# One weight block for the input and forget gates, and modulation sums that leave TensorE as columns

## The chip, the cores and the metric

The kernel runs on one core of one Trainium2 chip. The metric is the device time in microseconds (us) of one execution; three runs of the kernel before give 1740.52 us in the median (1740.15 to 1742.07).

## The reference

One step of a diffusion backbone with one layer on T = 640 tokens (128 of context, 512 latent) of D = 1024 features. What matters here is the modulation and the mixer's first product:

```python
mod = jax.nn.silu(cond) @ w_mod + b_mod            # cond: c for the latent tokens, c_ctx for the context
sh1, sc1, g1, shm, scm, gm, sh2, sc2, g2 = jnp.split(mod, N_MOD, axis=-1)
h = modulate(rmsnorm(x, norm_g[0]), sh1, sc1)
x = x + 0.5 * g1[:, None, :] * swiglu(h, ffn1_w1, ffn1_w2)
h = modulate(rmsnorm(x, norm_g[1]), shm, scm)
y, C, n, m = mixer(h, ...)                         # z = h @ w_in + b_in, 9232 columns
x = x + gm[:, None, :] * y
h = modulate(rmsnorm(x, norm_g[2]), sh2, sc2)
x = x + 0.5 * g2[:, None, :] * swiglu(h, ffn2_w1, ffn2_w2)
```

In `z`, 8 columns are the input gates (2 directions x 4 heads) and the 8 after them the forget gates. They feed the scans of the mLSTM; the other columns are q, k, v and o per head, the short convolution's inputs and two output gates.

## The kernel before

Everything is feature-major: x is eight tiles of 128 features x 640 tokens, and the tokens are worked in two halves of 320. TensorE (PE) does nearly all of it in products of 128 x 128 weights and 128 x 320 activations. For precision each operand is split into a high and a low part, so one product is three matmuls (`three`, L235 to L240: high*high, high*low, low*high). A block of 128 weight columns over 1024 rows thus costs 8 x 2 x 3 = 48 matmuls. Weights come by DMA from SyncE's queue (SP) into a ring of five raw tiles `wr` (L544 for the modulation, L195 for the rest, L1052 for the gates); ScalarE (ACT) casts the high part `wh` (L73) and VectorE (DVE) subtracts to the low part `wl` (L74), some four half-blocks ahead of their use. Sums of blocks `ws` (L211) are for Strassen's form, in which a pair of blocks takes seven products in place of eight (`pair_el`).

The program is a list of elements run in order; each engine executes its own instructions in the order in which the elements emit them. The parts that the change touches:

**Head of the mixer** (`head_el`, L340). Behind the second norm come three pairs of column blocks without Strassen: the two gate blocks (8 real columns each, the other 120 zeroed by GpSimd and loaded as four small DMAs, `gate_load`), then q and k of head 0. The left halves of the first three blocks are interleaved; then come the modulation products that `mid` holds (L582); then the right halves of these three blocks, then both halves of the other three. While PE does these, DVE and ACT make the sums and splits for Strassen's form of the same activations (the list `work`, 28 calls, L842 to L851 and L74), spread evenly over the units behind the first. The gates leave PSUM by `gate_ev` (L1083), one bias per partition; `gate0` and what follows, woven into the next four pairs, turn them into decays on DVE and ACT.

**Modulation on VectorE** (`mod_dve`, L649). Ten half-channels (512 columns of `w_mod`, two condition vectors) are computed by DVE: `acc += w * cm` (L668) into two accumulators per half (128 partitions x 512, or two pieces of 256), spread over other elements by `with_units`. The sum over partitions is then made by PE in four steps, an element apart: `red` (L676) multiplies each accumulator, as the moving operand, by two columns of the constant `sel`, giving two rows of 512 in PSUM; `mod_cols` copies them to SBUF (`rows_`, L557, two DVE copies), turns them into columns by four transposes on PE (`turn`, L562), and adds the bias (`put_`, L568) into `modT`. Half-channels whose products PE does itself (L582, L604, L629) go through `mod_cols` too.

In row names `ax` and `ps` are PSUM banks, `ma`, `x` and `HT1h`/`HT2h` the accumulators, `H..h`/`H..l` and `U..` split activations, `t` temporaries.

Of the kernel before, what the change touches and what calls it, by code (L numbers as in the profile page):

```python
# [44 lines left out]
def mixer_step(ctx: ExitStack, tc: tile.TileContext, x_prompt, x_sample, state_C, state_n, state_m,  # L45
# [30 lines left out]
    # ------------------------------------------------------------ program: weights run ahead of their use  # L76
# [122 lines left out]
    # ------------------------------------------------------------ products  # L199
    # One pair of 128-column blocks of weights against both token halves: seven products (Winograd's form  # L200
    # of Strassen's algorithm over column blocks, halves of the contraction and halves of the tokens).
# [46 lines left out]
    def relax(left=1):  # L248
        """Emit what can wait no longer, with this many calls to come."""
        while lazy and len(lazy) >= left:  # L250
            lazy.pop(0)()
# [46 lines left out]
    def pair_el(load1, load2, ev, e1=None, units=(), spare_v=False):  # L298
        """units: elements with operands of their own, put between the products."""
        po = pair_ops(e1=e1)  # L300
        at_ = {1 + 2 * i: u for i, u in enumerate(units)}
        loads, ops_ = [load1, load2], []
        for i, name in enumerate(ORDER):
            ops_.append(po[name])
            if i in at_:
                ops_ += [dict(o, raws=[len(loads)], src=(lambda t, c: lambda o: rtile[o["base"] + t][:, c:c + 512])(
                    len(loads), c)) for c, o in zip((0, 512), at_[i]["ops"])]
                loads += at_[i]["raws"]

        def emit():  # L310
            nf = len(fill)
            for i, _ in enumerate(pair_steps(ORDER, ev, spare_v)):
                if i in at_:
                    at_[i]["emit"]()
                relax(7 - i)
                drain(nf - nf * (i + 1) // 7)
        return dict(element(loads, ops_, emit), pair=True)
# [22 lines left out]
    def head_el(p, chain, work, mid=()):  # L340
        """The three pairs behind a norm, without Strassen: three left halves first, row block by row block as the
        norm yields them, then what mid holds, while the right halves are made."""
        pre = len(mid) // 2
        order = [None] * pre + [0, 1, 2] + [None] * (len(mid) - pre) + [3, 4, 5]
        at_ = {t: i for i, t in enumerate(order) if t is not None}

        def emit():
            flush()
            n = {"i": 0}

            def take(u, i):
                u["emit"](raw(el["base"] + i))
                rdone.add(el["base"] + i)
                load_more()

            def some(*_):
                n["i"] += 1
                if n["i"] == 3 and soon:
                    soon.pop(0)()
                while len(work) > 0 and n["i"] * total >= 18 * (total - len(work) + 1):  # L360
                    work.pop(0)()

            total = len(work)
            ev = lambda t: lambda h_, ps: p[t // 2][2](t % 2, h_, ps)
            hold()
            for i in range(pre):
                take(mid[i], i)
            w = [[op()] for t in range(3)]
            ps = [big() for t in range(3)]
            for k in range(KT):  # L370
                if k == 4:
                    for t in range(3):
                        w[t].append(op())
                for t in range(3):
                    three(ps[t][:, :HT], *w[t][k // 4], k % 4, plain_acts(k, 0), k == 0, k == KT - 1)
                if k == 3:
                    chain[0]()
                if k == 4:
                    chain[1]()
            for t in range(3):  # L380
                ev(t)(0, ps[t][:, :HT])
            chain[2]()
            for i in range(pre, len(mid)):
                take(mid[i], 3 + i)
            chain[3]()
            for t in range(3):
                unit(w[t], KT, plain_acts, 1, ev(t), {3: some, 7: some})
                release(2)
            for t in range(3, 6):
                w = [op(), op()]  # L390
                unit(w, KT, plain_acts, 0, ev(t), {3: some, 7: some})
                unit(w, KT, plain_acts, 1, ev(t), {3: some, 7: some})
            while work:
                work.pop(0)()
            for f in chain[4:]:
                f()
        loads = [p[t // 2][t % 2] for t in range(6)]
        loads = [u["raws"][0] for u in mid[:pre]] + loads[:3] + [u["raws"][0] for u in mid[pre:]] + loads[3:]
        oa = [dict(tile_ops(KT, at_[t])[i], raws=[at_[t]]) for i in range(2) for t in range(3)]
        ob = [dict(o, raws=[at_[t]]) for t in range(3, 6) for o in tile_ops(KT, at_[t])]  # L400
        el = dict(element(loads, oa + ob, emit), calm=True)
        return el

    def halves_el(loads, nk, acts, ev, after):
        """Column blocks whose left halves all come first, then their right halves."""
# [54 lines left out]
    # ------------------------------------------------------------ constants  # L460
# [15 lines left out]
    sel = cst.tile([P, 4], F32, name="sel")  # L476
    G.memset(sel, 0.0)
    G.memset(sel[:, 0:1], 1.0)
    G.memset(sel[:, 3:4], 1.0)
# [17 lines left out]
    gb = cst.tile([36, 2], F32, name="gb")  # L497
# [3 lines left out]
    for d in range(2):  # L501
        for i, off in enumerate((IG_OFF, FG_OFF)):
            G.dma_start(gb[32 * d:32 * d + 4, i:i + 1], dap(b_in, off + 4 * d, [[1, 4], [1, 1]]))
        G.dma_start(m0[32 * d:32 * d + 4, :], dap(state_m, 4 * d, [[1, 4], [1, 1]]))

    # Sums seeded by a copy into PSUM go on accumulating: every bank they use has been written by the PE once.
# [32 lines left out]
    # ------------------------------------------------------------ modulation  # L539
# [9 lines left out]
    def mod_cols(ch, m0_, n, p, parts):  # L549
        """Rows of the modulation to columns, in three steps."""  # L550
# [64 lines left out]
    def mod_mix(ch, half):  # L615
        """Half of a channel: units with split operands and units in float32 by turns."""
# [33 lines left out]
    def mod_dve(ch, halves, wide):  # L650
        units = []
        for half in halves:
            hold_ = {}
            for kq in range(4):
# [16 lines left out]
                def red(hold_=hold_):  # L671
                    p = aux()
                    n = 512 // len(hold_[0])
                    for j in range(len(hold_[0])):
                        for i in range(2):
                            PE.matmul(p[:2, j * n:j * n + n], sel[:, 2 * i:2 * i + 2], hold_[i][j], start=(i == 0),  # L676
                                      stop=(i == 1))
                    hold_["p"] = p

                def fin(ch=ch, half=half, hold_=hold_):  # L680
                    hold_["f"] = mod_cols(ch, 4 * half, 4, hold_["p"][:2, :], 1)
                    hold_["f"].pop(0)()

                def more(hold_=hold_):
                    hold_["f"].pop(0)()
                units.append((mod_load(ch, half, kq), fns, [red, fin, more, more] if kq == 3 else []))
        return units

    def with_units(main, units, spare=0):
        """Spread modulation units over elements; what a unit leaves to be done follows an element later."""  # L690
# [37 lines left out]
    # ------------------------------------------------------------ norms  # L728
# [87 lines left out]
    def right_chain(n, sh, first=False):  # L816
        """Steps in the order of head_el, and the sums of Strassen's algorithm that it makes by the way."""
# [63 lines left out]
    # ------------------------------------------------------------ feed-forward  # L881
    GROUPS = (6, 6, 6, 4)

    def ffn(w1, w2, g, norm_, lists, units, e1=None, mid=()):
        """Elements: [head], then per group the other pairs and the column blocks of w2."""
        head, els, f0 = [], [], 0
        for size in GROUPS:
            U = {}
            grp = []
            for j in range(size):  # L890
# [15 lines left out]
                if f0 + j < 3:  # L906
                    head.append(p)
# [28 lines left out]
    # ------------------------------------------------------------ start: x, first norm  # L936
# [83 lines left out]
    # ------------------------------------------------------------ mixer  # L1020
# [26 lines left out]
    def gate_load(off):  # L1047
        def load(t):
            G.memset(t, 0.0)
            r3_ = t.rearrange("p (k n) -> p k n", k=KT)  # L1050
            for d in range(2):
                nc.sync.dma_start(r3_[:, :, 32 * d:32 * d + 4],  # L1052
                                  dap(w_in, off + 4 * d, [[IN_COLS, P], [P * IN_COLS, KT], [1, 4]]))
        return load
# [25 lines left out]
    def gate_ev(mi, h, src):  # L1080
        if (mi, h) == (0, 0):
            GT["t"] = tp.tile([P, T], F32, name="sqacc")
        V.tensor_scalar(GT["t"][64 * mi:64 * mi + 36, hsl(h)], src[0:36, :], gb[:, mi:mi + 1], None, op0=OP.add)  # L1083
# [154 lines left out]
    def head_steps(h):  # L1238
# [103 lines left out]
        def rs_begin():  # L1342
            """The mean squares to the power -0.5, by Newton's iteration from an estimate on the bits."""
# [118 lines left out]
    prog.append(head_el([(gate_load(IG_OFF), gate_load(FG_OFF), gate_ev), h0[0], h0[1]], chain, work,  # L1462
# [16 lines left out]
    # ------------------------------------------------------------ output side of the mixer  # L1479
# [138 lines left out]
    # ------------------------------------------------------------ second feed-forward, output  # L1618
# [92 lines left out]
```

## Time and profile before

| | |
|---|---|
| median of 3 runs | 1740.52 us |
| the profiled execution: span from its first to its last instruction (the profile shows no other time of it) | 1743.3 us |
| PE busy | 1706.1 us, 98% of the span |
| PE weight loads | 1625.3 us, 93% |
| DVE busy | 1299.9 us, 75% |
| ACT busy | 814.4 us, 47% |
| mean granted TensorE clock | 0.995 |

Matmuls are pipelined: the duration of one in the profile is longer than the distance from its start to the next one's start, so costs on PE are read from starts, not from durations. The records of one fp32 matmul with an unsplit operand are two (18 calls of L757 are 36 records), each with its own weight load.

### The profile page before, as it was taken

The page shows a single profiled execution, that of the slowest core. Times are in us where ns is not written, and L with a number is a line of the kernel's source. Part 1 is how long each engine was busy: PE and PEld are TensorE (multiplying, and loading weights), DVE is VectorE, ACT ScalarE, POOL GpSimd, SP SyncE. Part 2 cuts the span into 40 slices and gives each one's busy share as a digit, 9 for nine tenths or more (in the row PEclk, how much of TensorE's full clock was granted, in tenths as well). Part 3 has the DMA queues.
Part 4 walks back from the last instruction along what each step waited for, and adds up shares of the span by engine and source line. Part 5 has one row for each costly group of instructions (what it writes and reads, how often), then busy time and mean ns, then how long its engine had stood idle before and what let it go on. Part 6 is the DMA issues. An engine that isn't in the chain of part 4 may idle for free.

```text
span 1743.3 us, 29445 instructions
## 1 busy us (share of the span) xinstructions
PE 1706.1 (98%) x11169; PEld 1625.3 (93%) x11169; DVE 1299.9 (75%) x2742; ACT 814.4 (47%) x1749; POOL 169.5 (10%) x253
## 2 busy tenths in 40 slices
PE   8899999999999999999999999999999999999997
PEld 3889999999989899999999999999989999999997
DVE  5787787786868868787887788869767567467476
ACT  5553352452554675564653255542255435245253
POOL 1010000000030122111102222001100000000001
PEclk9899999999999999999999999999999999999999
DMA  8335334343343443333328433347432322322222
GB/s 290 100 116 150 86 112 119 97 116 115 95 111 112 99 115 82 88 101 78 105 87 270 145 85 86 99 142 217 136 94 62 101 73 68 103 73 85 82 77 61
DMA packets 273501, 193.13 MB, mean 111 GB/s; under 512 B 12179, under 2 KB 248346, under 8 KB 273360
## 3 DMA queue, kind: packets, MB, share of 16 engines
q1 hardware_dynamic: 264112, 161.96, 32.1%
q0 software_dynamic: 8480, 28.63, 5.9%
q8 instruction: 88, 1.44, 0.4%
q10 hardware_dynamic: 768, 0.66, 0.1%
q14 instruction: 53, 0.43, 0.1%
HBM read 175.92 MB, written 15.31 MB: 110 GB/s over the span
## 4 chain that ended last, share of the span: by engine, by line
PE 82%; DVE 8%; ACT 5%; issue 3%; DMA 2%; POOL 0%; ACTq 0%; DVEq 0%; POOLq 0%
PE ps L238 25%; PE ps L239 25%; PE ps L240 25%; DVE wl L74 2%; ACT wh L73 1%; PE ax L1292 1%; PE ax L1323 1%; PE ax L676 1%; DMA wr<-in_w_mod_dram 1%; PE ax L1295 1%; PE ax L582 1%; DVE ws L211 1%; DVE t L1436 1%; DVE x L1448 0%; PE ax L1269 0%
## 5 line engine op out<-in xcount | busy, mean ns | idle before, releaser
L74 DVE TENSOR_TENSOR wl<-wr,wh 128x512 fp32r<-128x512 f32 (+1 forms) x444 | 290.9, 671 | 96.2 <-ACT wh L73 94.3
L73 ACT CAST wh<-wr 128x512 fp32r<-128x512 f32 (+1 forms) x444 | 258.5, 595 | 195.8 <-PE ps L239 159.0
L74 DVE TENSOR_TENSOR wl<-ws,wh 128x512 fp32r<-128x512 f32 x288 | 202.8, 705 | 62.0 <-ACT wh L73 61.5
L73 ACT CAST wh<-ws 128x512 fp32r<-128x512 f32 x288 | 175.0, 618 | 105.7 <-DVE ws L211 63.9
L238 PE MATMUL ps<-Uh,wh 128*128 128x320 f32 x704 | 218.7, 311 | 0.0
L239 PE MATMUL ps<-Ul,wh 128*128 128x320 f32 x704 | 217.1, 308 | 0.0
L240 PE MATMUL ps<-Uh,wl 128*128 128x320 f32 x704 | 217.0, 308 | 0.0
L870 DVE SCALAR_TENSOR_TENSOR x<-ps,modT,x 128x128 f32<-128x128 f32 (+2 forms) x216 | 82.7, 433 | 121.8 <-PE ps L240 121.8
L238 PEld LDWEIGHTS ps<-Uh,wh 128*128 128x128 f32 x704 | 132.1, 188 | 2.6 <-issue 2.6
L238 PE MATMUL ps<-HT4h,wh 128*128 128x320 f32 x392 | 124.6, 318 | 8.2 <-ACT t L284 3.6
L239 PEld LDWEIGHTS ps<-Ul,wh 128*128 128x128 f32 x704 | 132.1, 188 | 0.2 <-DVE Ul L74 0.2
L240 PEld LDWEIGHTS ps<-Uh,wl 128*128 128x128 f32 x704 | 132.1, 188 | 0.0
L238 PE MATMUL ps<-H11h,wh 128*128 128x320 f32 x392 | 124.2, 317 | 1.7 <-ACT H11h L73 1.7
L239 PE MATMUL ps<-HT4l,wh 128*128 128x320 f32 x392 | 122.2, 312 | 0.7 <-DVE HT4l L74 0.7
L239 PE MATMUL ps<-H11l,wh 128*128 128x320 f32 x392 | 122.4, 312 | 0.1
L238 PE MATMUL ps<-H21h,wh 128*128 128x320 f32 x392 | 122.4, 312 | 0.0
L240 PE MATMUL ps<-H11h,wl 128*128 128x320 f32 x392 | 122.1, 311 | 0.0
L240 PE MATMUL ps<-HT4h,wl 128*128 128x320 f32 x392 | 122.1, 311 | 0.0
L240 PE MATMUL ps<-H21h,wl 128*128 128x320 f32 x392 | 121.3, 310 | 0.2 <-DVE wl L74 0.2
L239 PE MATMUL ps<-H21l,wh 128*128 128x320 f32 x392 | 121.1, 309 | 0.0
L238 PE MATMUL ps<-H22h,wh 128*128 128x320 f32 x360 | 113.0, 314 | 0.0
L240 PE MATMUL ps<-H22h,wl 128*128 128x320 f32 x360 | 111.7, 310 | 0.0
(380 smaller groups left out, 4560.0 us busy)
## 6 DMA issues: line engine op xcount, KB each, us to landing
wr<-in_ffn_w_dram SPq DMA_DIRECT2D x88, 512.0 KB, 3.9
wr<-in_w_mod_dram SPq DMA_DIRECT2D x72, 512.0 KB, 3.8
wr<-in_w_in_dram SPq DMA_DIRECT2D x72, 512.0 KB, 3.9
wr<-in_ffn_w_dram SPq DMA_DIRECT2D x48, 384.0 KB, 3.5
wr<-in_ffn_w_dram SPq DMA_DIRECT2D x16, 256.0 KB, 2.9
wr<-in_w_ml_out_dram SPq DMA_DIRECT2D x8, 512.0 KB, 5.0
wr<-in_w_sc_out_dram SPq DMA_DIRECT2D x8, 512.0 KB, 4.1
wr<-in_w_o_dram SPq DMA_DIRECT2D x8, 512.0 KB, 4.5
```

The costliest lines, as they stand in the source:

```text
L73: A.copy(hi, raw)
L74: V.tensor_sub(lo, raw, f32(hi))
L211: getattr(engine, fn)(t, part(o, a), part(o, b))
L238: PE.matmul(ps, hi[:, ws], ah, start=start, stop=False, skip_group_check=True)
L239: PE.matmul(ps, hi[:, ws], al, start=False, stop=False, skip_group_check=True)
L240: PE.matmul(ps, lo[:, ws], ah, start=False, stop=stop, skip_group_check=True)
L582: PE.matmul(hold["p"][:2, :], cm[:, 2 * kq + k, :], w[:, 512 * k:512 * k + 512], start=(kq == 0 and k == 0), stop=(kq == 3 and k == 1))
L676: PE.matmul(p[:2, j * n:j * n + n], sel[:, 2 * i:2 * i + 2], hold_[i][j], start=(i == 0), stop=(i == 1))
L870: V.scalar_tensor_tensor(X[m][:, o + a:o + b], ps[:, a:b], modT[:, g, m, cd:cd + 1], X[m][:, o + a:o + b], op0=OP.mult, op1=OP.add)
L1292: PE.matmul(p2[:, :DH + 1], S["q", dt][:, sl], S["C"][d][:, dt, :], start=(dt == 0), stop=(dt == 1))
L1295: PE.matmul(p1[:, :DH + 1], S["p", ch][:, d, :], PO["vt"][:, ch, :], start=True, stop=True)
L1323: PE.matmul(p[:, :DH + 1], kw[:, dt * P:(dt + 1) * P], PO["vt"][:, ch, :], start=True, stop=True)
```

## The change

Two edits.

*Gates.* One weight tile holds both gate blocks: the input gates of the two directions in columns 0 and 32, the forget gates in columns 64 and 96. `head_el` takes a list of single blocks, here the gate block and the four of q and k, and spreads `work` over the units that are left (`points = 4 * nb - 6`: 14 for five blocks, 18 for six). The gates leave PSUM in one instruction per half, 100 partitions tall, with `gb` a single column.

*Modulation.* In `mod_dve` each 128-column piece of an accumulator becomes the stationary operand, and one column of ones the moving one: eight matmuls give a [128, 8] result that is already in columns. `sel`, the copies and the transposes go, and `fin` adds the bias straight from PSUM.

```diff
-    def head_el(p, chain, work, mid=()):
-        pre = len(mid) // 2
-        order = [None] * pre + [0, 1, 2] + [None] * (len(mid) - pre) + [3, 4, 5]
+    def head_el(blocks, chain, work, mid=()):
+        pre, nb = len(mid) // 2, len(blocks)
+        order = [None] * pre + [0, 1, 2] + [None] * (len(mid) - pre) + list(range(3, nb))
+        points = 4 * nb - 6
...
-                while len(work) > 0 and n["i"] * total >= 18 * (total - len(work) + 1):
+                while len(work) > 0 and n["i"] * total >= points * (total - len(work) + 1):
                     work.pop(0)()
...
-            for t in range(3, 6):
+            for t in range(3, nb):
                 w = [op(), op()]
                 unit(w, KT, plain_acts, 0, ev(t), {3: some, 7: some})
                 unit(w, KT, plain_acts, 1, ev(t), {3: some, 7: some})
...
-    gb = cst.tile([36, 2], F32, name="gb")
+    gb = cst.tile([100, 1], F32, name="gb")
...
                 def red(hold_=hold_):
-                    p = aux()
+                    p = hold_["p"] = aux()
                     n = 512 // len(hold_[0])
-                    for j in range(len(hold_[0])):
+                    for j in range(4):
+                        a = j * P % n
                         for i in range(2):
-                            PE.matmul(p[:2, j * n:j * n + n], sel[:, 2 * i:2 * i + 2], hold_[i][j], start=(i == 0),
-                                      stop=(i == 1))
-                    hold_["p"] = p
+                            PE.matmul(p[:, 2 * j + i:2 * j + i + 1], hold_[i][j * P // n][:, a:a + P], ones[:, 0:1],
+                                      start=True, stop=True)

                 def fin(ch=ch, half=half, hold_=hold_):
-                    hold_["f"] = mod_cols(ch, 4 * half, 4, hold_["p"][:2, :], 1)
-                    hold_["f"].pop(0)()
-
-                def more(hold_=hold_):
-                    hold_["f"].pop(0)()
-                units.append((mod_load(ch, half, kq), fns, [red, fin, more, more] if kq == 3 else []))
+                    b0 = ch * KT + 4 * half
+                    V.tensor_add(modT[:, ch, 4 * half:4 * half + 4, :],
+                                 hold_["p"][:, :8].rearrange("p (a b) -> p a b", a=4),
+                                 bmT[:, b0:b0 + 4, None].to_broadcast([P, 4, 2]))
+                units.append((mod_load(ch, half, kq), fns, [red, fin] if kq == 3 else []))
...
-    def gate_load(off):
-        def load(t):
-            G.memset(t, 0.0)
-            r3_ = t.rearrange("p (k n) -> p k n", k=KT)
+    def gate_load(t):
+        G.memset(t, 0.0)
+        r3_ = t.rearrange("p (k n) -> p k n", k=KT)
+        for i, off in enumerate((IG_OFF, FG_OFF)):
             for d in range(2):
-                nc.sync.dma_start(r3_[:, :, 32 * d:32 * d + 4],
+                c0 = 64 * i + 32 * d
+                nc.sync.dma_start(r3_[:, :, c0:c0 + 4],
                                   dap(w_in, off + 4 * d, [[IN_COLS, P], [P * IN_COLS, KT], [1, 4]]))
...
-    def gate_ev(mi, h, src):
-        if (mi, h) == (0, 0):
+    def gate_ev(h, src):
+        if h == 0:
             GT["t"] = tp.tile([P, T], F32, name="sqacc")
-        V.tensor_scalar(GT["t"][64 * mi:64 * mi + 36, hsl(h)], src[0:36, :], gb[:, mi:mi + 1], None, op0=OP.add)
+        V.tensor_scalar(GT["t"][0:100, hsl(h)], src[0:100, :], gb, None, op0=OP.add)
...
-    prog.append(head_el([(gate_load(IG_OFF), gate_load(FG_OFF), gate_ev), h0[0], h0[1]], chain, work,
+    prog.append(head_el([(gate_load, gate_ev)] + blocks_of(h0[0]) + blocks_of(h0[1]), chain, work,
                         mod_pe(GM, (0,), False)))
```

How the instructions move. On PE, at the first `red` of the program (the last products of the first feed-forward's group, then those of the next pair), before:

```order
L240 MATMUL ps<-Uh,wl 128x320
L676 MATMUL ax<-ma,sel 2x512 x2
L238 MATMUL ps<-H11h,wh 128x320
L239 MATMUL ps<-H11l,wh 128x320
L240 MATMUL ps<-H11h,wl 128x320
```

and with the change:

```order
L240 MATMUL ps<-Uh,wl 128x320
L677 MATMUL ax<-ones,ma 128x1 x8
L238 MATMUL ps<-H11h,wh 128x320
L239 MATMUL ps<-H11l,wh 128x320
L240 MATMUL ps<-H11h,wl 128x320
```

The place is the same; two matmuls of 512 columns have become eight of one column, and the four transposes (L562) that stood some products later are gone.

On DVE, in the head of the mixer from the last modulated right half on (HT4l and H22l are the right halves' low parts, L842 or L841 the first of `work`, `sqacc` the gates' rows), before:

```order
L842 TENSOR_TENSOR Ul<-Ul 128x320
L842 TENSOR_TENSOR Uh<-Uh 128x320
L842 TENSOR_TENSOR Ul<-Ul 128x320
L1083 TENSOR_SCALAR sqacc<-ps,gb 36x320
L74 TENSOR_TENSOR wl<-wr,wh 128x512 x2
L557 COPY t_6189<-ax 2x256
L557 COPY t_6190<-ax 2x256
L842 TENSOR_TENSOR Uh<-Uh 128x320
L74 TENSOR_TENSOR HT1l<-Ul,HT1h 128x320
L74 TENSOR_TENSOR HT1l<-Uh,HT1h 128x320
L1083 TENSOR_SCALAR sqacc<-ps,gb 36x320
```

and with the change:

```order
L841 TENSOR_TENSOR Ul<-Ul 128x320
L841 TENSOR_TENSOR Uh<-Uh 128x320
L841 TENSOR_TENSOR Ul<-Ul 128x320
L841 TENSOR_TENSOR Uh<-Uh 128x320
L1083 TENSOR_SCALAR sqacc<-ps,gb 100x320
L74 TENSOR_TENSOR wl<-wr,wh 128x512 x2
L557 COPY t_6173<-ax 2x256
L557 COPY t_6174<-ax 2x256
L74 TENSOR_TENSOR HT1l<-Ul,HT1h 128x320
L74 TENSOR_TENSOR HT1l<-Uh,HT1h 128x320
L74 TENSOR_TENSOR HT1l<-Ul,HT1h 128x320
L74 TENSOR_TENSOR HT1l<-Uh,HT1h 128x320
```

Per unit of PE there is more of `work`, and the second eviction of a gate block is gone (the L557 here is that of a half-channel that PE computes itself, which stays).

On SP, the loads of the head (the gates, L1052 or L1053, then q of head 0), before:

```order
L544 DMA wr<-in_w_mod_dram 128x2x512 x2
L1052 DMA wr<-in_w_in_dram 128x8x4 x4
L195 DMA wr<-in_w_in_dram 128x8x128
L544 DMA wr<-in_w_mod_dram 128x2x512 x2
```

and with the change:

```order
L544 DMA wr<-in_w_mod_dram 128x2x512 x2
L1053 DMA wr<-in_w_in_dram 128x8x4 x4
L195 DMA wr<-in_w_in_dram 128x8x128 x2
L544 DMA wr<-in_w_mod_dram 128x2x512 x2
```

The gates take one raw tile in place of two, so the second block of q is loaded ahead of the second pair of modulation loads.

## Rows read from the trace of the kernel before

**Rows 1.** The page of the kernel before: busy time, share of the span and instructions per engine.

```profile
PE 1706.1 (98%) x11169; PEld 1625.3 (93%) x11169; DVE 1299.9 (75%) x2742; ACT 814.4 (47%) x1749; POOL 169.5 (10%) x253
```

**Rows 2.** The page: the chain of work that ended last, by engine.

```profile
PE 82%; DVE 8%; ACT 5%; issue 3%; DMA 2%; POOL 0%; ACTq 0%; DVEq 0%; POOLq 0%
```

**Rows 3.** Busy time of each engine by stretch: the stretch, its length, then busy us and instruction counts of PE, PEld (weight loads), DVE, ACT and POOL, the granted clock (1.00 is 2.4 GHz, 0.50 is 1.2 GHz), the DMA engines' mean busy share and GB/s. The stretches are the first feed-forward behind its first group, the head's left halves, the head from its second modulation products to its last unit, the pairs with the gates' chain behind it, and a piece of those.

```profile
150.00:490.00 340.00, 340.00 (x2274) 330.23 (x2274) 259.81 (x492) 132.54 (x276) 0.96 (x1) 1.00 0.38 109
516.00:530.00 14.00, 13.76 (x87) 11.83 (x86) 11.58 (x29) 8.08 (x20) 3.50 (x7) 1.00 0.98 328
528.80:566.40 37.60, 37.60 (x241) 34.44 (x241) 30.02 (x66) 18.46 (x41) 0.00 (x0) 1.00 0.28 75
...
579.00:600.00 21.00, 17.31 (x103) 16.26 (x102) 20.31 (x37) 11.83 (x22) 3.11 (x9) 0.92 0.23 67
591.80:595.20 3.40, 3.40 (x15) 3.40 (x14) 3.33 (x7) 0.62 (x1) 0.00 (x0) 0.50 0.00 0
```

**Rows 4.** PE in order of time around the first `red`: start, us, engine, line, operation, count. Between the first two rows shown stand 19 more matmuls of the same kind.

```profile
184.72 0.31 PE L238 MATMUL ps<-Uh,wh 128*128 128x320 f32 x1
...
187.66 0.31 PE L240 MATMUL ps<-Uh,wl 128*128 128x320 f32 x1
187.89 1.88 PE L676 MATMUL ax<-ma,sel 128*2 128x512 f32 x4
189.70 0.41 PE L238 MATMUL ps<-H11h,wh 128*128 128x320 f32 x1
189.96 0.30 PE L239 MATMUL ps<-H11l,wh 128*128 128x320 f32 x1
```

**Rows 5.** The same around one `turn`.

```profile
214.30 0.31 PE L240 MATMUL ps<-HT4h,wl 128*128 128x320 f32 x1
214.54 0.40 PE L562 MATMUL ax<-ident,t 2*128 2x2 f32 x4
214.87 0.41 PE L238 MATMUL ps<-H11h,wh 128*128 128x320 f32 x1
215.12 0.31 PE L239 MATMUL ps<-H11l,wh 128*128 128x320 f32 x1
```

**Rows 6.** The same around the last `red`, which its `turn` follows at once.

```profile
1258.93 0.31 PE L240 MATMUL ps<-HT4h,wl 128*128 128x320 f32 x1
1259.17 1.02 PE L676 MATMUL ax<-HT1h,sel 128*2 128x256 f32 x4
...
1261.57 0.61 PE L562 MATMUL ax<-ident,t 2*128 2x2 f32 x4 [0.51 <-DVE t L557]
1262.11 0.42 PE L238 MATMUL ps<-H11h,wh 128*128 128x320 f32 x1
1262.36 0.31 PE L239 MATMUL ps<-H11l,wh 128*128 128x320 f32 x1
```

**Rows 7.** Groups of PE's instructions by line: records, busy us, mean ns, idle time before them.

```profile
L676 PE MATMUL ax<-ma,sel 128*2 128x512 f32 x20 | 9.4, 592 | 0.0
L676 PE MATMUL ax<-x,sel 128*2 128x512 f32 x8 | 3.8, 592 | 0.0
L676 PE MATMUL ax<-HT2h,sel 128*2 128x256 f32 x12 | 3.1, 379 | 0.0
L676 PE MATMUL ax<-HT1h,sel 128*2 128x256 f32 x12 | 3.1, 378 | 0.0
```

**Rows 8.** PE in order of time around the three matmuls of the second norm's statistics (L757): a 128 x 128 fp32 tile stationary, two columns moving.

```profile
521.06 0.31 PE L240 MATMUL ps<-H11h,wl 128*128 128x320 f32 x1
521.21 0.72 PE L757 MATMUL ax<-ones,sqacc 128*128 128x2 f32 x6
521.79 0.39 PE L238 MATMUL ps<-H21h,wh 128*128 128x320 f32 x1
522.02 0.31 PE L239 MATMUL ps<-H21l,wh 128*128 128x320 f32 x1
```

**Rows 9.** All records of L757: count, duration ns (min/median/max).

```profile
L757 PEld LDWEIGHTS ax<-ones,sqacc x36: 186/192/192, 501.8 to 1735.0; 128*128 128x128 f32 x36
L757 PE MATMUL ax<-ones,sqacc x36: 167/251/272, 501.8 to 1735.1; 128*128 128x2 f32 x36
```

**Rows 10.** What PE waited for at L676, over the whole run (us, times): the largest of its waits for DVE.

```profile
  DVE x L870: 0.7, 2
```

**Rows 11.** DVE (count, duration ns, first and last start): the copies of the modulation's rows and the evictions of the gates over the whole run, and the low parts of unsummed weights between 529 and 567 us.

```profile
L557 DVE COPY t<-ax x28: 401/404/412, 121.1 to 1310.7; 2x256 f32<-2x256 f32 x24, 4x256 f32<-4x256 f32 x4
L1083 DVE TENSOR_SCALAR sqacc<-ps,gb x4: 535/544/545, 528.9 to 539.8; 36x320 f32<-36x320 f32 x4
L74 DVE TENSOR_TENSOR wl<-wr,wh x8: 673/686/693, 536.6 to 559.0; 128x512 fp32r<-128x512 f32 x8
```

**Rows 12.** DVE in order of time: the first two sums of `work`, and at the end of the head the eviction of the last unit (k of head 0), the first instruction after the last sums; in brackets the idle time before it and what ended that.

```profile
534.15 0.48 DVE L842 TENSOR_TENSOR Ul<-Ul 128x320 f32<-128x320 f32 x1
534.55 0.48 DVE L842 TENSOR_TENSOR Uh<-Uh 128x320 f32<-128x320 f32 x1
...
564.33 0.55 DVE L1214 TENSOR_SCALAR x<-ps,biT 128x320 f32<-128x320 f32 x1 [1.37 <-PE ps L240]
```

**Rows 13.** PE in order of time in the second pair behind the head: its longest wait there.

```profile
588.60 0.31 PE L240 MATMUL ps<-H22h,wl 128*128 128x320 f32 x1
590.74 0.41 PE L238 MATMUL ps<-HT4h,wh 128*128 128x320 f32 x1 [1.83 <-ACT t L284]
```

More of the change, by code (lines that the diff above doesn't have):

```diff
@@ L359, in some @@
                     soon.pop(0)()
-                while len(work) > 0 and n["i"] * total >= 18 * (total - len(work) + 1):
+                while len(work) > 0 and n["i"] * total >= points * (total - len(work) + 1):
                     work.pop(0)()
             total = len(work)
-            ev = lambda t: lambda h_, ps: p[t // 2][2](t % 2, h_, ps)
+            ev = lambda t: lambda h_, ps: blocks[t][1](h_, ps)
             hold()
@@ L396, in emit, with blocks_of @@
                 f()
-        loads = [p[t // 2][t % 2] for t in range(6)]
+        loads = [b[0] for b in blocks]
         loads = [u["raws"][0] for u in mid[:pre]] + loads[:3] + [u["raws"][0] for u in mid[pre:]] + loads[3:]
         oa = [dict(tile_ops(KT, at_[t])[i], raws=[at_[t]]) for i in range(2) for t in range(3)]
-        ob = [dict(o, raws=[at_[t]]) for t in range(3, 6) for o in tile_ops(KT, at_[t])]
+        ob = [dict(o, raws=[at_[t]]) for t in range(3, nb) for o in tile_ops(KT, at_[t])]
         el = dict(element(loads, oa + ob, emit), calm=True)
         return el
+    def blocks_of(p):
+        return [(p[i], lambda h, ps, i=i: p[2](i, h, ps)) for i in range(2)]
     def halves_el(loads, nk, acts, ev, after):
@@ L475, in mixer_step @@
     V.tensor_scalar(mask[:, 1, :], jp, 0.0, NEG, op0=OP.is_gt, op1=OP.mult)
[L476 to L479, printed above, removed]
     cvec = st.tile([16, P], F32, name="cvec")
@@ L502, in mixer_step @@
         for i, off in enumerate((IG_OFF, FG_OFF)):
-            G.dma_start(gb[32 * d:32 * d + 4, i:i + 1], dap(b_in, off + 4 * d, [[1, 4], [1, 1]]))
+            G.dma_start(gb[64 * i + 32 * d:64 * i + 32 * d + 4, :], dap(b_in, off + 4 * d, [[1, 4], [1, 1]]))
         G.dma_start(m0[32 * d:32 * d + 4, :], dap(state_m, 4 * d, [[1, 4], [1, 1]]))
@@ L906, in ffn @@
                 if f0 + j < 3:
-                    head.append(p)
+                    head.extend(blocks_of(p))
                 else:
@@ L1045, in mixer_step @@
     R = {}
-    def gate_load(off):
-        def load(t):
-            G.memset(t, 0.0)
-            r3_ = t.rearrange("p (k n) -> p k n", k=KT)
+    def gate_load(t):
+        G.memset(t, 0.0)
+        r3_ = t.rearrange("p (k n) -> p k n", k=KT)
+        for i, off in enumerate((IG_OFF, FG_OFF)):
             for d in range(2):
-                nc.sync.dma_start(r3_[:, :, 32 * d:32 * d + 4],
+                c0 = 64 * i + 32 * d
+                nc.sync.dma_start(r3_[:, :, c0:c0 + 4],
                                   dap(w_in, off + 4 * d, [[IN_COLS, P], [P * IN_COLS, KT], [1, 4]]))
-        return load
     def spill_x():
```

## The prediction

> **What bounds the kernel now.** I read the page first: PE is busy for 98% of the span and DVE for 75% [rows 1], and the chain of waits lies for 82% on PE [rows 2]. The view by stretch then tells where this holds. From 150 to 490 us PE is busy for 340.0 of 340.0 us at full clock, with DVE at 259.8 [rows 3]: a PE microsecond saved there is one saved at the end. In the head of the mixer (528.8 to 566.4) PE is busy throughout as well, and DVE for 30.0 of 37.6 us. Only in the two pairs behind it (579 to 600) is DVE the tight engine, 20.3 of 21.0 us, while PE has 17.3 [rows 3]. So I price PE by the distance between starts (a matmul's duration overlaps the next one), and then ask whether DVE can follow.
>
> PE's unit of price: twenty steps from 184.72 to 187.66 are 0.147 us each [rows 4], for one product of 128 x 320.
>
> **The gates.** A block is 48 such matmuls, so one block less is 48 x 0.147 = **7.05 us** off PE. With it go two casts on ACT and two subtractions of about 0.69 us on DVE, and two of four evictions of 0.544 us on DVE [rows 11]; one eviction of 100 partitions in place of 36 has the same 320 columns, so I keep 0.544 for it. DVE's list in the head falls from 30.0 to about 30.0 - 2 x 0.69 - 2 x 0.54 = 27.5 us, while the stretch shrinks from 37.6 to 30.5 [rows 3]. It fills nine tenths of its time where it filled eight. It must be level again by the head's last eviction, and in the trace DVE stood idle for 1.37 us before that one, waiting for PE [rows 12]. In the new order 34 operations of up to 320 columns and 11 of 512 stand on DVE from the first sum of `work` to that eviction: at 0.40 us from start to start [rows 12] and at most 0.69 [rows 11] these are about 21 us, and from 534.15 to 564.33 - 7.05 there are 23.1. DVE is level again, though with 2 us in hand, not 10. So I take the whole 7.05. If that cover is gone, the last splits (HT4) come late; they feed only the seventh product of the next pair, six products of 12 x 0.147 = 1.76 us later, so this small lateness would not stop PE, and what would is the rival below.
>
> On the queues, SP issues the same four small loads, and POOL clears one tile in place of two; neither is waited for. The second block of q now is loaded before the second modulation loads, ahead of the stretch where the DMA engines are 98% busy (516 to 530) [rows 3], instead of in it; one slot of the ring further on, later loads keep their distance to their use. I take 0 for it.
>
> **The modulation, removed.** Around a `red` the second product after it starts at 189.96, the last before it at 187.66; less two steps of 0.147, the `red` costs 2.30 - 0.29 = **2.01 us** [rows 4]. (I count to the second product since the first one after such a piece is followed late.) A `turn` costs in the same way 215.12 - 214.30 - 0.29 = **0.53 us** [rows 5]. There are ten half-channels: 20 + 8 + 24 records of `red` [rows 7], where seven have 4 records of 512 columns and three 8 of 256. The last has `red` and `turn` together, with a wait of 0.51 us for DVE's copies: 1262.36 - 1258.93 - 0.29 = 3.14 us [rows 6]. I take 2.01 for the other 256-column ones too, since they stream the same number of columns. Sum: 9 x (2.01 + 0.53) + 3.14 = **26.0 us** of PE. Of DVE's copies 20 x 0.404 = 8.1 us go [rows 11], all in stretches where PE is the limit: nothing on the path. The eviction that adds the bias stays, one per half.
>
> **The modulation, added.** Each half now takes eight matmuls of a 128 x 128 fp32 stationary tile and one moving column. The trace has nearly this operation: three matmuls with such a tile and two moving columns, six records, delay the products by 522.02 - 521.06 - 0.29 = 0.67 us, so 0.111 us per record [rows 8]. Sixteen records are 16 x 0.111 = 1.78 us, and ten halves **17.8 us**. Lower bound: a record cannot be cheaper than nothing, 0 us; that would gain 17.8 us more. Upper bound: load and matmul of every record one after the other, 0.192 + 0.251 = 0.443 us [rows 9], 70.9 us in ten halves. I take 0.111, because the row differs only by one moving column, and both ends are far from what six records in a row do. A wait of PE for the accumulators was possible before as well; its largest wait for DVE at L676 was 0.7 us in all [rows 10], and the order leaves `red` in its place an element after the last accumulation. `fin` then stands on DVE where the first copy stood, so nothing queues behind it that did not.
>
> **Sum.** 7.05 + 26.0 - 17.8 = 15.2 us. Against the profiled execution, 1743.3 - 15.2 = 1728.1; its span lies 2.8 us above the median of the runs, which ends at 1740.5 - 15.2 = **1725.3 us**.
>
> **Rivals.**
> *The clock falls.* PE stood still from 588.6 to 590.7 [rows 13], and the clock was at 0.50 (1.2 GHz) from 591.8 to 595.2 [rows 3]: 1.7 us lost. A `red` of 1.78 us now streams 16 columns where it streamed 2048; should the chip take this for idleness, some of the ten would cost 1.7 us more each: with two to four of them 1728.7 to 1732.1. Against it: the stop at 588.6 was longer, and PE keeps loading weights.
> *The head gives nothing.* DVE is the limit from 579 on [rows 3]; if it leaves the head seven microseconds behind, PE waits for it in the next pairs and only the modulation's 8.2 us are left: 1732.4. Against it is DVE's idle time before the last eviction [rows 12].
> *A record paced by its own load*, 0.192 us [rows 9]: `red` is 3.07, ten are 30.7; 7.05 + 26.0 - 30.7 = 2.3 gained, 1738.2, no change that can be told.
> *Slower: loads that don't overlap.* All stationary tiles here fill the array; if the load of the next accumulator piece starts only when the matmul before it has ended, a record costs 0.443 us and the ten `red` 70.9: 1740.5 + 70.9 - 33.05 = 1778. It decides at 33.05 / 160 = 0.207 us per record; above that the kernel gets slower. Against it: six records, each with a load of 0.19 and a matmul of 0.25 us [rows 9], fit into 0.67 us [rows 8]. This is also what the Trainium skill's page "TensorE: Matmul & The Clock Gate" (Part 3, "The mechanism") says: loads overlap matmuls in flight "only when row_grp differs". By that rule this change loses. The trace disagrees with it: loads are busy for 1625 us beside 1706 of matmuls [rows 1].
> That the change doesn't do what it says has no room: the order shows 8 matmuls in place of 2 and no transposes, and 48 products fewer.
>
> **How the numbers follow.** Forecast 0.66; clock 0.15; head 0.11; load-paced 0.05; slower 0.03. A difference of 0.2% (3.5 us) is about what can be told from none. The first three are all faster by more: 0.92; load-paced is the same: 0.05; slower 0.03. The forecast's own range is 1722 to 1728: the runs differ by 2 us, and the half-clock piece at 591.8 may go, come back elsewhere, or double. The range over the first three, 1722 to 1733, leaves out the last two and a little of the tails.
>
> **What would show it.** Right: per half one group of 16 records on L677 that delays products by about 1.8 us; no L562 at those places; the head from the second modulation products to the last unit 30.5 us long; PE's waits behind it as before (about 4 us in the two pairs). Wrong: records of L677 at 0.19 us or more apart; a clock of 0.50 behind a `red`; more PE waits for DVE's low parts or sums between 550 and 600 us.

## The result

The changed kernel takes 1726.80 us in the median of four runs (1725.98 to 1728.00), beside 1740.34 of before (1740.01 to 1742.07): ratio 0.9918, interval 0.9904 to 0.9932. By the medians that is 13.5 us. Measured twice more (experiments 3 and 12), the ratio was 0.9899 (0.9883 to 0.9915) and 0.9904 (0.9888 to 0.9921). The forecast of 15.2 us is a ratio of 0.9913 and lies in all three intervals.

The page of the changed kernel, busy time and chain of waits:

```profile
PE 1689.7 (98%) x11189; PEld 1627.5 (94%) x11189; DVE 1291.2 (75%) x2718; ACT 813.4 (47%) x1747; POOL 168.8 (10%) x249
PE 84%; DVE 7%; ACT 4%; issue 2%; DMA 1%; ACTq 0%; DVEq 0%; POOL 0%
```

PE is busy 16.4 us less than in [rows 1], and still for 98% of a shorter span; DVE is busy 8.7 us less, 7.4 of them the copies (L557: 10.3 before, 2.9 now). PE's weight loads are busy 2.2 us more: 160 came with the column sums, and 140 went (48 of the gates' block, 52 of the old sums in L676 and 40 of the transposes in L562), hence the 20 more on the page.

The first `red` and the last one, as PE ran them (start, us, engine, line, operation, count):

```profile
185.84 0.31 PE L240 MATMUL ps<-Uh,wl 128*128 128x320 f32 x1
185.98 1.84 PE L677 MATMUL ax<-ones,ma 128*128 128x1 f32 x16
187.69 0.40 PE L238 MATMUL ps<-H11h,wh 128*128 128x320 f32 x1
187.92 0.31 PE L239 MATMUL ps<-H11l,wh 128*128 128x320 f32 x1
...
1242.96 0.31 PE L240 MATMUL ps<-HT4h,wl 128*128 128x320 f32 x1
1243.11 0.95 PE L677 MATMUL ax<-ones,HT1h 128*128 128x1 f32 x8
1243.92 1.03 PE L677 MATMUL ax<-ones,HT2h 128*128 128x1 f32 x8
1244.81 0.39 PE L238 MATMUL ps<-H11h,wh 128*128 128x320 f32 x1
1245.05 0.30 PE L239 MATMUL ps<-H11l,wh 128*128 128x320 f32 x1
```

Counted as in [rows 4], a `red` delays the products by 187.92 - 185.84 - 0.29 = 1.79 us (2.01 before), and the last one by 1245.05 - 1242.96 - 0.29 = 1.80 (3.14 before, [rows 6]). There is no other work on PE at a place like that of [rows 5].

The records of L677 in `ma` and their waits: count, duration ns (min/median/max), first and last start.

```profile
L677 PEld LDWEIGHTS ax<-ones,ma x80: 187/192/192, 185.8 to 476.3; 128*128 128x128 f32 x80
L677 PE MATMUL ax<-ones,ma x80: 164/250/250, 186.0 to 476.3; 128*128 128x1 f32 x80
```

They are as long as those of [rows 9], and sixteen loads and matmuls fit into 1.79 us, though every load fills the array. The line of the Trainium skill ("TensorE: Matmul & The Clock Gate", Part 3, "The mechanism") by which a load overlaps a matmul in flight only on another row group does not hold for them. The same section also lets a load into a background weight buffer go ahead; the overlap here is at odds with the first statement and not with the second, and the trace cannot show which buffer was used.

Busy time by stretch (columns as in [rows 3]): the first feed-forward, the head from its second modulation products to its last unit, the pair behind, and the next two pairs.

```profile
150.00:490.00 340.00, 340.00 (x2340) 340.00 (x2339) 258.80 (x490) 134.31 (x278) 1.83 (x2) 1.00 0.38 110
523.40:554.00 30.60, 30.60 (x194) 27.57 (x193) 27.48 (x63) 16.64 (x40) 0.00 (x0) 1.00 0.27 72
554.00:566.60 12.60, 12.57 (x86) 12.31 (x85) 9.47 (x17) 8.44 (x15) 0.00 (x0) 1.00 0.32 83
566.60:588.00 21.40, 15.91 (x103) 14.86 (x102) 20.71 (x38) 11.90 (x23) 3.51 (x9) 1.00 0.24 68
```

The head is 30.6 us long (forecast 30.5) with DVE busy for 27.48 (forecast 27.5). In the next two pairs DVE is busy for 20.7 of 21.4 us where it was for 20.3 of 21.0, and PE for 15.9 where it was for 17.3.

### The profile page after: what moved, and what is told of

Read it like the earlier page. It is cut to its first block, busy times and chain, and to the rows that moved or that the text cites. A ratio compares the mean times of both kernels' runs of the same rounds, so it can differ in the third digit from the quotient of the medians.

```text
span 1726.1 us, 29446 instructions
## 1 busy us (share of the span) xinstructions
PE 1689.7 (98%) x11189; PEld 1627.5 (94%) x11189; DVE 1291.2 (75%) x2718; ACT 813.4 (47%) x1747; POOL 168.8 (10%) x249
## 4 chain that ended last, share of the span: by engine, by line
PE 84%; DVE 7%; ACT 4%; issue 2%; DMA 1%; ACTq 0%; DVEq 0%; POOL 0%
PE ps L238 26%; PE ps L239 25%; PE ps L240 25%; DVE wl L74 2%; PE ax L1292 1%; PE ax L1323 1%; ACT wh L73 1%; PE ax L677 1%; PE ax L1295 1%; PE ax L582 1%; DVE ws L211 1%; DVE t L1436 1%; DVE x L1448 0%; PE ax L1269 0%; DMA out_dram<-Cc 0%
```

## The experiments

Two numbers serve throughout: the times of the runs, and the distance between the same two products in two traces. The second is sharper, since the first 125 to 130 us (DMA of x and the first modulation) vary from one execution to the next: the product that starts at 129.03 in the first trace of before starts at 126.64 in a second one, and between 124.40 and 129.90 in the other kernels' traces, whose program up to there is nearly the same. From that product to the last one:

| kernel | to the product, us | from it to the last product, us |
|---|---|---|
| before, first and second trace | 129.03, 126.64 | 1603.35, 1603.44 |
| gates alone | 125.83 | 1593.74 |
| modulation alone | 125.20 | 1592.74 |
| both (three traces) | 127.20, 124.63, 126.62 | 1587.84, 1585.99, 1585.98 |

The code shows each edit against the changed kernel, the longer ones in part.

**1. Gates alone.** `red`, `fin` and `sel` as before, the gates as changed.

```diff
-                units.append((mod_load(ch, half, kq), fns, [red, fin] if kq == 3 else []))
+                units.append((mod_load(ch, half, kq), fns, [red, fin, more, more] if kq == 3 else []))
```

> Only the gates' half of the change; the modulation's sums stay as rows with copies and transposes. My theory (each part by its own PE time): 48 products less, 7.05 us, so about 1733.3 against 1740.3, and the head from its second modulation products to its last unit is 30.5 us long in place of 37.6. Rival (the change's 1.6 us that are missing from 15.2 are lost behind the head, where VectorE is the limit): 5.4 us gained, 1734.9.

Measured: 1732.38 against 1741.18, ratio 0.9944 (0.9929 to 0.9958); by the ratio 9.7 us with an interval of 7.3 to 12.4. Three products, one in the middle of the head, the first behind the head, and the second of the third pair there, before:

```profile
545.36 0.31 PE L239 MATMUL ps<-H21l,wh 128*128 128x320 f32 x1
566.42 0.31 PE L238 MATMUL ps<-HT1h,wh 128*128 128x320 f32 x1
599.27 0.42 PE L238 MATMUL ps<-HT2h,wh 128*128 128x320 f32 x1 [1.06 <-ACT ps L266]
```

and with the gates alone:

```profile
542.12 0.31 PE L239 MATMUL ps<-H21l,wh 128*128 128x320 f32 x1
556.13 0.31 PE L238 MATMUL ps<-HT1h,wh 128*128 128x320 f32 x1
588.99 0.41 PE L238 MATMUL ps<-HT2h,wh 128*128 128x320 f32 x1 [1.06 <-ACT ps L266]
```

Between the first two there are 14.02 us in place of 21.06: 7.04 us, as priced. Nothing of it is given back behind the head: from the second to the third it is 32.85 us here and 32.86 before. The 9.6 us of the table hold 2.6 more, which fell away near 920 us (experiments 3 and 4).

**2. Modulation alone.** The gates keep two blocks.

```diff
-    prog.append(head_el([(gate_load, gate_ev)] + blocks_of(h0[0]) + blocks_of(h0[1]), chain, work,
+    prog.append(head_el([(gate_load(IG_OFF), gate_load(FG_OFF), gate_ev), h0[0], h0[1]], chain, work,
```

> Only the modulation's half; the gates keep two blocks. My theory: ten half-channels at 2.54 us less 1.78, and the last one's wait: 8.2 us gained, 1732.1 against 1740.3, with 1.78 us per group of sixteen records. Rival (part of the gain is lost at the waits for VectorE and DMA downstream): 6.6 us or less.

Measured: 1732.12, ratio 0.9946 (0.9929 to 0.9964); by the ratio 9.4 us with an interval of 6.3 to 12.4. The five half-channels of the first feed-forward shorten their stretch from 416.3 to 412.53 us, and the five after 919 us from 800.40 to 796.06: 3.8 + 4.3 = 8.1 us (forecast 8.2). Here too the table has 2.6 us more, at the same place near 920.

**3 and 4. Both again, and before again.** No edit.

> The changed kernel once more, on the chip and beside the runs of before that the two halves are compared with. My theory: 15.2 us gained, ratio 0.9913, the sum of the two halves within 1 us. Rival: 13.6 us gained, ratio 0.9922, and the sum of the halves is larger than the whole.

> The kernel before, once more, for a second trace of it. If the profiled execution of before was a slow one by its start and by waits that come and go (its span 1743.3 is longer than the times of three of its runs), this span is 1738 to 1741, and the places where the two traces of before differ lie before 130 us and between 590 and 1000. If the difference of 17.2 us between the two spans is what the change does, this span is 1743 again.

Measured: 1724.81 against 1741.18, ratio 0.9899. The second trace of before has a span of 1741.1 us in place of 1743.3, and nearly all of the difference lies before the product of the table. The places that were changed add up: 7.0 + 3.8 + 4.3 = 15.1 us. The traces show 17.4 us (1603.4 to 1586.0), or 15.5 in the first trace of the changed kernel. The 2.3 more are waits of PE that fell away in the scans of the mixer (between about 600 and 925 us), where no instruction was changed. They fell away in the traces of either half alone as well, so the whole distances of the two halves (9.6 and 10.6 us) add up to 20.2, more than both together give. In the two traces of before, and in two of the changed kernel, the waits that differ most are

```profile
914.70 0.42 PE L238 MATMUL ps<-HT2h,wh 128*128 128x320 f32 x1 [0.63 <-ACT ps L266]
924.24 0.42 PE L238 MATMUL ps<-HT4h,wh 128*128 128x320 f32 x1 [1.74 <-ACT t L284]
```

```profile
652.02 0.70 PE L1295 MATMUL ax<-vt,pt 128*128 128x257 f32 x2 [0.99 <-ACT Cc L1328]
913.47 0.41 PE L238 MATMUL ps<-HT2h,wh 128*128 128x320 f32 x1 [0.39 <-ACT ps L266]
921.95 0.41 PE L238 MATMUL ps<-HT4h,wh 128*128 128x320 f32 x1 [0.67 <-ACT t L284]
```

```profile
642.16 0.70 PE L1295 MATMUL ax<-vt,pt 128*128 128x257 f32 x2 [1.29 <-ACT Cc L1328]
907.13 0.42 PE L238 MATMUL ps<-HT3h,wh 128*128 128x320 f32 x1 [0.24 <-ACT ps L276]
```

```profile
902.75 0.42 PE L238 MATMUL ps<-HT3h,wh 128*128 128x320 f32 x1 [0.24 <-ACT ps L276]
906.81 0.42 PE L238 MATMUL ps<-HT4h,wh 128*128 128x320 f32 x1 [0.28 <-ACT t L284]
```

The wait near 650 stands in one trace of either kernel, so it comes and goes. Those near 920 for the products of HT2h and HT4h were longer in both traces of before (2.4 and 1.1 us) than in any of the twelve others (0 to 0.8). What ends the longest is a transfer: PE waits for a copy on ACT (L284) that stands behind a cast, and the cast waits for data that GpSimd sends out to device memory and back (`rd`). In the first trace of before:

```profile
922.53 0.82 ACT L73 CAST Bh<-x 128x320 fp32r<-128x320 f32 x2 [2.17 <-DMA x<-rd]
923.77 0.41 ACT L284 COPY t<-ps 128x320 f32<-128x320 f32 x1
```

ACT's wait for this transfer is 2.2 and 1.1 us in the traces of before and 0.6 to 1.2 in the others. Whether the change shortens it, by an earlier arrival, or two traces are too few, stays open.

**5. Every column sum twice in a row.** 32 records per group.

```diff
-                    for j in range(4):
+                    for j in (0, 1, 2, 3, 0, 1, 2, 3):
```

> The changed kernel with every column sum made twice (the second time over the first, same result): ten groups of 32 records in place of 16. My theory (0.111 us per record, paced by the loads of the stationary tiles): 1.78 us more per group, 17.8 in all, which uses up the whole gain: about 1743 against 1741 of before. Rival (the clock falls where PE streams next to no columns for 3.6 us): the clock stands at 0.50 behind some of the ten groups, up to 1.7 us more for each.

Measured: 1758.84 against 1741.95, ratio 1.010 (1.0084 to 1.0115): 33 us more than the changed kernel, not the 17.8 of the records alone. From the product of the table to the end it is 1619.20 us, 33.2 more. The groups cost 1.79 us more each, and the clock does what the rival said. The first group, and busy time (columns as in [rows 3]) of the piece behind it:

```profile
184.65 3.63 PE L677 MATMUL ax<-ones,ma 128*128 128x1 f32 x32
188.14 0.40 PE L238 MATMUL ps<-H11h,wh 128*128 128x320 f32 x1
```

```profile
189.30:192.70 3.40, 3.40 (x15) 3.40 (x14) 0.94 (x2) 0.94 (x2) 0.00 (x0) 0.50 0.03 7
```

There are 15 products in 3.4 us, where 23 fit at full clock. Such a piece stands behind nine of the ten groups (the fifth's is twice as long), and the 15.3 us beyond the records are 1.5 us per piece.

**6. 24 records per group**, in the same way, to see how near the change is to that.

```diff
-                    for j in range(4):
+                    for j in (0, 1, 2, 3, 0, 1):
```

> Six of the eight column sums... twelve matmuls, 24 records per group in place of 16, 2.7 us: how near the changed kernel is to the point where the clock falls. By the records alone 8.9 us more than the changed kernel, about 1734. If the clock already falls at this length behind some groups, a clock of 0.50 shows behind them and up to 1.7 us more for each.

Measured, one run: 1744.24, 19 us above the changed kernel, where the records alone make 8.9. The clock is at 0.50 behind seven of the ten groups, the first among them:

```profile
184.45 2.73 PE L677 MATMUL ax<-ones,ma 128*128 128x1 f32 x24
187.04 0.40 PE L238 MATMUL ps<-H11h,wh 128*128 128x320 f32 x1
```

```profile
187.60:191.00 3.40, 3.40 (x14) 3.40 (x14) 0.00 (x0) 0.79 (x2) 0.00 (x0) 0.50 0.46 136
```

From the product of the table to the end it is 1605.64, 19.7 more than the changed kernel: 8.9 and 1.5 for each of the seven.

**7. The same 32 records, an element apart.** The second 16 follow when products have run in between.

```diff
-                units.append((mod_load(ch, half, kq), fns, [red, fin] if kq == 3 else []))
+                units.append((mod_load(ch, half, kq), fns, [red, again, fin] if kq == 3 else []))
```

> Every column sum is made twice as in the kernel with 32 records, but the second group of 16 stands one element after the first, with products between them. If the loss beyond 17.9 us was the clock (a long stretch with next to no moving columns), no clock of 0.50 stands behind the groups here and the run takes 17.9 us more than the changed kernel: about 1743, level with before. If it was something else in the second set of records, it is again about 1758.

Measured: 1743.80 against 1742.24, ratio 1.0006 (0.9997 to 1.0016): 18.3 us more than the changed kernel (1725.54 beside it). Nine of the ten pairs of groups have no fall behind them. The tenth does, at 1262.3 us, and that one pair was not apart: at the end of the list both groups are emitted at once.

```profile
1258.50 0.95 PE L680 MATMUL ax<-ones,HT1h 128*128 128x1 f32 x8
1259.30 1.03 PE L680 MATMUL ax<-ones,HT2h 128*128 128x1 f32 x8
1260.20 1.03 PE L680 MATMUL ax<-ones,HT1h 128*128 128x1 f32 x8
1261.09 1.03 PE L680 MATMUL ax<-ones,HT2h 128*128 128x1 f32 x8
```

With the same 32 records, then, the clock fell behind nine of ten unbroken groups and behind none of the nine that were split: here the unbroken length made the difference, not the number of records. Behind groups of 16 (1.79 us) no trace shows a fall: three of the changed kernel and five of its variants, 80 groups.

**8 and 9. More work on DVE in the head.** Idle subtractions of 320 columns, 12 and 24 of them, spread over `work`.

```diff
+        if sh == SHM:
+            def extra():
+                if "xtra" not in N:
+                    N["xtra"] = t3()
+                V.tensor_sub(N["xtra"], N[0, 7], N[0, 6])
+            for i in range(12):
+                work.insert(2 + i * 24 // 12 + i, extra)
```

> The changed kernel with 12 idle subtractions of 320 columns more on VectorE in the head of the mixer, about 0.40 us each, 4.8 us. My theory: about 1 us of them fits in before the last eviction, some 3 us more into the idle time of the pair behind (12.6 us long, 9.5 busy), so PE loses at most 1 us up to the end of the two pairs. Rival (DVE is full in the head, lateness goes through): PE loses 3.8 us or more there.

> The same with 24 subtractions, 9.6 us. My theory: about 4 us are absorbed, so PE reaches the end of the stretch with the gates' chain 5 to 6 us later than in the changed kernel: the point from which the gates' gain is given back. Rival (PE waits only for the split sums, which have 10 us to spare): 1 us or less. Other rival: nothing is absorbed, 8.6 us.

Measured, one run each: 1726.78 and 1729.16. With 12 the head and the pairs behind it are as long as without (14.02 and 32.85 us between the three products of experiment 1, against 14.02 and 33.12): 4.8 us on DVE cost nothing. With 24 they are 15.80 and 35.70: 4.4 us lost of 9.6, a little less than the 5 to 6 expected. The stretch of the head in the two kernels:

```profile
523.80:554.40 30.60, 30.60 (x194) 27.45 (x194) 29.82 (x70) 16.01 (x37) 0.00 (x0) 1.00 0.27 73
```

```profile
521.70:552.30 30.60, 29.41 (x190) 27.04 (x188) 29.81 (x69) 13.61 (x31) 0.00 (x0) 1.00 0.26 69
```

DVE is full in both, 29.8 of 30.6 us, and only in the second does PE wait, at the start of the pair behind:

```profile
552.73 0.38 PE L238 MATMUL ps<-HT1h,wh 128*128 128x320 f32 x1 [1.62 <-DVE x L1221]
557.23 0.41 PE L238 MATMUL ps<-HT2h,wh 128*128 128x320 f32 x1 [2.52 <-ACT ps L266]
```

The first wait is for an eviction (L1221 is this kernel's L1214): PE goes on when DVE has emptied that PSUM bank. The second and longer one is for a copy on ACT, and ACT was held up by the last sums of `work` (L850), which it casts first. ACT in order of time:

```profile
554.27 0.46 ACT L73 CAST HT4h<-Ul 128x320 fp32r<-128x320 f32 x1 [4.07 <-DVE Ul L850]
556.76 0.42 ACT L266 COPY ps<-ps 128x320 f32<-128x320 f32 x1
```

The splits of HT4 themselves are not waited for: the seventh product starts at 564.56 without a wait.

**10. Work off DVE behind the head.** The gates' copies, one subtraction and the sums S1 and S3 of three pairs to GpSimd, one memset less.

```diff
-        V.tensor_copy(f_, GT["t"][64:100, :])
+        G.tensor_copy(f_, GT["t"][64:100, :])
...
-        V.tensor_sub(R["i"], R["i"], b)
+        G.tensor_sub(R["i"], R["i"], b)
...
-    prog += weave([pair_el(*j, spare_v=True) for j in (h0[2], gml_pair(0), h1[0], h1[1])],
+    prog += weave([pair_el(*j, G if i else None, spare_v=True)
+                   for i, j in enumerate((h0[2], gml_pair(0), h1[0], h1[1]))],
```

> The changed kernel with work taken off VectorE behind the head: the gates' two copies and one subtraction go to GpSimd, one memset of 0.6 us goes, and the weight sums S1 and S3 of the second to fourth pair go to GpSimd (0.7 us each on VectorE). Theory: VectorE sets the pace there (20.7 of 21.4 us busy, PE 15.9), so some 2.4 us of the chain and 2 to 3 us of sums come back: 3 to 5 us faster than the changed kernel, 1720 to 1722 where the changed one takes 1725. Rival (the chain's own length and the table loads of ScalarE set the pace, or GpSimd's operations are slow enough to hold the weights back): no gain or a loss.

Measured: 1729.82 against 1741.95, ratio 0.9935 (0.9921 to 0.9948): slower than the changed kernel by some 4 us (4.8 from the product of the table to the last one), so the rival held. GpSimd runs in order too: a weight sum stands behind a DMA issue that waits 5.50 us for another transfer to land, the cast on ACT waits for the sum, and the copy that PE waits for stands behind the cast. GpSimd, ACT and PE, each in order of time:

```profile
598.62 0.57 POOL L1177 DMA_DIRECT2D decB<-decd  x1 [5.50 <-DMA decd<-sm_de]
599.21 1.27 POOL L211 TENSOR_TENSOR ws<-wr 128x512 f32<-128x512 f32 x1
```

```profile
600.52 0.62 ACT L73 CAST wh<-ws 128x512 fp32r<-128x512 f32 x1 [2.70 <-POOL ws L211]
601.04 0.42 ACT L266 COPY ps<-ps 128x320 f32<-128x320 f32 x1
```

```profile
601.51 0.41 PE L238 MATMUL ps<-HT2h,wh 128*128 128x320 f32 x1 [2.32 <-ACT ps L266]
```

**11 and 12. Only the copies and the memset, beside the changed kernel.** The first edit of the kernel above for both copies, and

```diff
-        V.tensor_copy(d0[:, 2 * P:T:P], bl[:, 1:4])
-        V.memset(d0[32:36, :], 0.0)
+        V.tensor_copy(d0[:32, 2 * P:T:P], bl[:32, 1:4])
```

> The changed kernel with less work on VectorE behind the head, and none of the late GpSimd work of the kernel before: only the gates' two copies go to GpSimd (idle there, 1.1 us each) and one memset of 0.6 us goes. If VectorE's list sets the pace there, 1.0 to 1.6 us faster than the changed kernel in the stretch behind the head, at the limit of what the runs can tell. Rival: the chain of the gates through ScalarE sets the pace, and the stretch is as long as before.

> The changed kernel a third time, beside the lighter one on the same chip. By my sum the ratio to before is 0.991 (15.2 us); the two measurements so far gave 0.9918 and 0.9899.

Measured: 1725.00 (ratio 0.9901, 0.9886 to 0.9916) and 1725.54 (0.9904, 0.9888 to 0.9921): no difference that the runs can tell. The stretch behind the head is 32.34 us in place of 33.13, so about half of the 1.6 us of DVE work came back.

## Why the prediction was right

The forecast of 15.2 us is the sum of two parts, and each was measured by itself at its place: 15.1 us. The single measurements of the whole (13.5 to 16.7 us by the medians) are too coarse to tell this sum from one that is 1 us off.

- *Gates, 7.05 us:* 7.04 in the trace, alone and together with the other half.
- *Modulation, 26.0 off and 17.8 on:* per half-channel 2.01 + 0.53 less 1.79. The bounds were far apart (0 and 70.9 us), and the row that was nearest, three matmuls of L757, gave the price within 1%: a record takes 0.111 us from start to start whether one column or two follow, which points at the load of the 128 x 128 tile as what sets the pace. The Trainium skill's page "TensorE: Matmul & The Clock Gate" ("LDWEIGHTS") has a load take its columns divided by 1.2, in ns, an estimate of 107 ns for 128; these records agree within 4%. The transposes of before do not: their loads have 128 columns too, on 2 partitions, and follow each other every 0.06 us.

```profile
214.53 0.32 PEld L562 LDWEIGHTS ax<-ident,t 2*128 2x128 f32 x4 [0.19 <-issue]
```

- *DVE's room in the head:* too small in the forecast. It said 2 us in hand; DVE did stand idle for 1.0 us before the last eviction, yet 4.8 us more cost nothing, since the pair behind has idle time as well. The cost when the cover is gone was put in the wrong place: experiment 9 shows that PE does not wait at the seventh product for the splits of HT4, but earlier, for an eviction and for a copy on ACT that stands behind the late casts.
- *The clock piece at 591.8, put at 1.7 us:* this price was wrong. In two traces of the changed kernel the clock does not fall there, in the third it does (at 578.3), and the stretch from the second to the third product of experiment 1 is as long each time (33.12, 33.12 and 33.13 us). DVE sets the end of that stretch (1.6 us less work on DVE made it 0.8 us shorter, experiment 11); at full clock PE waits instead:

```profile
578.08 0.41 PE L238 MATMUL ps<-HT4h,wh 128*128 128x320 f32 x1 [1.84 <-ACT t L284]
583.53 0.42 PE L238 MATMUL ps<-HT1h,wh 128*128 128x320 f32 x1 [1.67 <-DVE t L290]
```

- *Rivals:* the head gave all its gain, the records are paced at 0.111 and overlap their loads. The clock rival named a real mechanism that this change stays short of: experiments 5 and 6 show falls behind groups of 2.7 and 3.6 us, at 1.5 us each where the rival had 1.7. Of the two reasons against it one did not hold: in them too PE keeps loading weights, and the clock falls all the same. That 16 records are few enough was not worked out ahead; that this rival did not come true is in part luck.
- *The profiled difference of 17.2 us* is not the change alone: 2 us lie in the start and in waits that differ between executions of one kernel.

## What to carry to other kernels

Where PE is busy throughout, price both sides of an exchange by what they delay the next products, in starts: a result that comes out as columns saves the copies and transposes behind it, and can be worth many small matmuls. Keep such matmuls in short groups with dense products between them: here 16 records at a time cost only themselves, 24 and 32 cost the clock as well. And ask of every loss, a slow clock among them, which engine sets the end of that stretch: if it is another one, the loss costs nothing, and mending it gains nothing.

## What the runs showed of the hardware

A stream of fp32 matmuls with one moving column, each with its own 128 x 128 load, keeps PE's queue busy without a gap, and yet the granted clock went from 1.00 to 0.50 (2.4 to 1.2 GHz) behind it: behind none of 80 groups of 1.79 us, seven of ten of 2.7 us, and nine of ten of 3.6 us, for 1.5 us each. GpSimd took 1.25 to 1.68 us (median 1.30, experiment 10) for a sum of 128 x 512 that takes DVE about 0.7.
